# Moving work around two stage boundaries of a hybrid encoder block: token differences, operand splits and the loads of the second branch

## The chip, the cores and the metric

The kernel runs on one core of a Trainium2 chip. The metric is device time in microseconds (us). Every time below comes from runs on the chip or from one execution that the hardware profiler recorded. The core has five instruction streams that run side by side and wait for one another only through semaphores: PE (matrix multiply), ACT (one-input functions), DVE (two-input elementwise work), POOL (a second elementwise engine) and SP, which in this kernel only issues DMAs. Each stream runs its own instructions strictly in order.

## The reference

One sub-layer takes `x` (1024 tokens by 1024 channels, float32). `h = rms_norm(x)` is multiplied by one wide matrix; its columns feed three mixers:

```
h = rms_norm(x, g_pre)
a_qkv, bq, bk, bv, mq, ga, gb, gm, mg = split(h @ w_in)
oa = dilated window attention of 3 groups (dilation 1, 4, 16), merged by softmax of their log-denominators
ob = softmax(qb kb^T / 8) vb          # grouped queries, qk-RMSNorm, axial rotary positions
om = softmax(mq km^T / sqrt(128)) vm  # cross-attention into 256 memory rows
ya, yb, ym = (oa*silu(ga)) @ w_br_a, (ob*silu(gb)) @ w_br_b, (om*silu(gm)) @ w_br_m
gates = sigmoid(mg + b_merge)
out = (gates[0]*ya + gates[1]*yb + gates[2]*ym) @ w_out
x = x + rms_norm(out, g_post)
```

In this text A is the dilated branch (`oa`), B the grouped-query branch (`ob`, "the second branch") and M the memory branch.

## The kernel before, in words

All matrix products keep float32 accuracy by writing each operand as a sum of a high and a low part and adding three matmuls (high times high, low times high, high times low). Making the two parts is a "split" (L104 to L106): one ACT copy that rounds to the high part, then one DVE subtraction for the low part. `hh[k]` and `hl[k]` hold the two parts of `x` times its norm gain, transposed, 128 channels for each k, all 1024 tokens.

The stages that matter here follow one another on PE:

1. Attention of B, woven with gate units. Its last lines, L792 to L795, load the softmax denominators of B (`lbd`, in DRAM) into the tile `rl`, take the reciprocal on DVE and store it to `rld` in DRAM. `rld` is read much later, where B's output is normalised (L1186).
2. The value stage, a list of 44 steps of 12 matmuls each (L966 to L1022). Steps 0 to 15 make the values of one group directly: two halves of the tokens, eight k each, with weights `v_first[k]`. Steps 16 to 43 make the values of the other two groups together by a Strassen-like scheme: seven products (`PRODUCTS`, L817) of four k each, in the order A11, A12, S2, S3, S4, S1, A22, where S1 to S4 are sums of weights (`sum_at`, POOL, L900) and T1 to T4 are differences of token blocks. The token differences are made from a fresh copy of `xT`: `x_load(k)` fetches two tiles of 512 KB into the two buffers named `wr`, `x_scale(k)` multiplies them by the gain on ACT (L838), `x_blocks(k)` forms four differences on DVE (L845) in the tiles `vv` or `vy` and stores each to DRAM as `tsd` (SP, L846). `blocks_at` (L877) loads them back from step 19 on, `split_at` splits weights and differences two steps ahead of their use, `v_store` (L903, L904) and `v_evac` (L909 to L924) take the results out of PSUM.
3. The query and key stage, with gates (L1088): the same seven products for 26 pairs of weight units, in an `order` written out by hand. T1, T2 and T3 are kept for it: `t_load` fetches T2 and T3 again in the value stage, and `tasks` (L1213 on) splits them during the first products of pair 0. `own_blocks(1)` splits the weights of pair 1.
4. The attention of A, twelve items of four steps (`q`, 48 in all), woven with the branch products (`fill`, L1292). In each step ACT computes exponentials (L1454) of scores that DVE masked (L1446); PE transposes them one step later (L1470, L1479) and multiplies them with values (L1499). The function `other` (L1602 on) places side work: `b_load(k)` fetches one of the four finished operand tiles of B into a buffer named `ot` (two buffers), and `b_split(k)` splits it into `hh[k+4]`, `hl[k+4]` with one ACT and one DVE instruction of 1024 elements. The branch products use these tiles after the eight units of M, that is from the 193rd of their matmul positions on.

From the value stage to the end of stage 4 the order of ACT, DVE, POOL, SP and PE is the order in which the program text names the instructions (`manual_schedule`, L802). So an instruction of step n that waits for a DMA holds back everything of later steps on its engine, however ready that is.

In a step of the value stage the program text names things in this order: the 12 matmuls; a split of `v_first` (for steps 2 to 5); `x_scale`; `split_at`; the evacuations of the product before; `blocks_at`; `sum_at`; `x_blocks` and `x_load`.

Of the kernel before, what the change touches and what calls it, by code (L numbers as in the profile page):

```python
# [8 lines left out]
F32 = mybir.dt.float32  # L9
# [8 lines left out]
P = 128  # L18
# [32 lines left out]
def block(ctx: ExitStack, tc: tile.TileContext, x, xT, memT, cst, msk, bcst, tabA, gpost,  # L51
          wu, wv, wb, wmem, wbr, wout, out):
    nc = tc.nc
# [611 lines left out]
    with tc.tile_pool(name="ba", bufs=1, reuse_waits="tile") as ba:  # L665
# [123 lines left out]
            add_filler(j)  # L789
        early[len(queue)] = first_values  # L790
        weave(len(FILL) - 1, b_att(), B_COST, B_LEAD, B_PRIO)
        rl = ba.tile([P, 64], F32, name="rl")  # L792
        nc.sync.dma_start(rl, lbd.rearrange("h (a b) -> (h a) b", b=64))
        V.reciprocal(rl, rl)
        nc.sync.dma_start(rld.rearrange("h (a b) -> (h a) b", b=64), rl)  # L795

    close(qp)
    close(kvp)
# [32 lines left out]
    def x_load(k):  # L831
        XT[:] = [wp.tile([P, S], F32, name="wr", bufs=WR) for _ in range(2)]
        for j, t in enumerate(XT):
            nc.sync.dma_start(t, xT[k + 4 * j])

    def x_scale(k):
        for j, t in enumerate(XT):
            A.activation(t, t, AF.Copy, scale=cs[:, C_GP + k + 4 * j:C_GP + k + 4 * j + 1])  # L838
# [7 lines left out]
            nc.sync.dma_start(tsd[j, k], to[j])  # L846

    x_load(0)
    VR = {}
    VT = {"A11": "ac0", "A21": "ac1", "A12": "ac2", "A22": "vA22"}  # L850
    for nm, u, kh in (("A21", 1, 0), ("A11", 0, 0), ("A22", 1, 1), ("A12", 0, 1)):
# [8 lines left out]
    def parts_of(t):  # L860
        return t[:, lo], t[:, hi]
# [113 lines left out]
    for n, (i, e, k) in enumerate(steps_v):  # L975
        if k == 0:
            now = v_banks()
        for j in range(4):
            if i is None:
                t = slice(e * 512 + j * 128, e * 512 + j * 128 + 128)  # L980
                (bh, bl), w, end = (hh[k][:, t], hl[k][:, t]), v_first[k], 7
            else:
                (bh, bl), w, end = tokens_at(i, k, j), SB[i, k], 3
            wh_, wl_ = parts_of(w)
            for q, (a, b) in enumerate(((bh, wh_), (bl, wh_), (bh, wl_))):
                PE.matmul(now[j], a, b, start=k == 0 and q == 0, stop=k == end and q == 2)
        behind = left.pop(0)() if left else []
        if n + 2 < 8 and n + 2 >= 4:
            v_first.append(slots0[n - 2])
            split(*parts_of(v_first[-1]), raw1[:, n - 2])  # L990
        if n < 16 and n % 4 == 2:
            x_scale(n // 4)
        m = n + 2 - FIRST
        if 0 <= m < 28:
            split_at(*divmod(m, 4))
        for f in behind:
            f()
        m = n + 5 - FIRST
        if 0 <= m < 28:
            blocks_at(*divmod(m, 4))  # L1000
        for nm, s0 in (("S1", 7), ("S3", 11), ("S2", 17), ("S4", 21)):
            if 0 <= n - s0 < 4:
                sum_at(nm, n - s0)
        if n < 16 and n % 4 == 3:
            x_blocks(n // 4)
            if n < 15:
                x_load(n // 4 + 1)
        if n == FIRST + 10:
            for j in range(2):
                nc.sync.dma_start(tab[j], tabA[:, j])  # L1010
        if n == FIRST + 17:
            V.tensor_tensor(tab[0], tab[0], rb, op=OP.mult)
            G.tensor_tensor(tab[1], tab[1], rb, op=OP.mult)
        if n == FIRST + 16:
            load_pair(0, 0)
            load_pair(0, 1)
        if n == FIRST + 21:
            own_blocks(0)
        if n - FIRST in (15, 16):
            t_load("T2", T2, n - FIRST - 15)  # L1020
        if n - FIRST in (19, 23):
            t_load("T3", T3, (n - FIRST - 19) // 4)  # L1022
        if k == end:
            for j in range(4):
                if i is None:
                    left.append(lambda b=now[j], T=4 * e + j: [lambda: v_store(rs(), VG[0], T, b)])
                else:
                    left.append(lambda i=i, j=j, b=now[j]: v_evac(i, j, b))
# [179 lines left out]
    def tasks(n, x):  # L1208
        if n < 2:
            blocks = {(0, "1"): [(0, "S1"), (0, "S2")], (0, "4"): [(0, "S3")], (1, "1"): [(1, "S1")], (0, "5"): [(0, "A22")],  # L1210
                      (1, "4"): [(0, "S4")], (0, "7"): [(1, "S2")], (0, "6"): [(1, "S3")], (1, "3"): [(1, "A22")],
                      (1, "2"): [(1, "S4")], (1, "5"): [(2, "S1")], (1, "7"): [(2, "S3")], (1, "6"): [(2, "A22")]}.get((n, x), ())
        else:  # L1213
            blocks = {"1": [(n, "S2")], "2" if n < last else "3": [(n, "S4")]}.get(x, [])
            if n < last:
                blocks = {"7": [(n + 1, "S3")], "6": [(n + 1, "A22")], "5": [(n + 1, "S1")]}.get(x, blocks)
        for m, nm in blocks:
            block_of(m, nm)
        for nm, k in {(0, "1"): [("T2", 0), ("T2", 1), ("T2", 2), ("T2", 3)], (0, "2"): [("T3", 0), ("T3", 1), ("T3", 2)],
                      (0, "4"): [("T3", 3)]}.get((n, x), ()):  # L1220
            split_block(nm, k)
        j = {(0, "2"): 1, (0, "4"): 2, (0, "3"): 3, (1, "4"): 4}.get((n, x))
        if j:
            weight_sum(1, j, SF)
        if n == 0:
            if x == "5":
                for u in range(2):
                    load_pair(2, u)
        elif n < last:
            if x == "3":  # L1230
                own_blocks(n + 1)
            j = {"4": 1, "3": 2, "2": 3, "5": 4}.get(x) if n > 1 else {"3": 1, "2": 2, "5": 3}.get(x)
            if j:
                weight_sum(n + 1, j, SF)
            if n == 1 and x == "5":
                weight_sum(2, 4, SF)
            if x == ("4" if n > 1 else "3") and n + 2 <= last:
                load_pair(n + 2, 0)
                load_pair(n + 2, 1)
        if x in "325":  # L1240
            for u, y in ((1, "3"), (0, "2")):
                if x == y:
                    rope_add(n - 1, u)
            for u, y in ((1, "2"), (0, "5")):
                if x == y:
                    rope_store(n - 1, u)
        if n == last - 1 and x in "46" or n == last and x == "1":
            if x != "6":
                m_load(wp.tile([P, S], F32, name="wr", bufs=WR))
            if x != "1":  # L1250
                m_load(sr.tile([P, S], F32, name="rw", bufs=2))
        if n == last and x in "4352":
            for k in (0, 1) if x in "45" else (2, 3):
                t = lo if x in "43" else hi
                split(hh[k][:, t], hl[k][:, t], MB[k][:, t])
# [105 lines left out]
    with tc.tile_pool(name="aa", bufs=1, reuse_waits="tile") as aa:  # L1361
# [169 lines left out]
        def b_load(k):  # L1531
            GG[1, k] = aa.tile([P, S], F32, name="ot", bufs=2)
            nc.sync.dma_start(GG[1, k], od[1, k])

        def b_split(k):
            split(hh[k + 4], hl[k + 4], GG.pop((1, k)))
# [73 lines left out]
        def other(n, j):  # L1610
            p_, g = divmod(n, 3)
            if j == 2:
                if n + 2 < len(items):
                    qk_load(n + 2)
                if n + 1 < len(items):
                    items[n + 1]["values"]()
            if g == 0 and n:
                if j == 0:
                    COM[p_] = combine(p_ - 1)
                    COM[p_]["fetch"]()  # L1620
                elif j == 2:
                    COM[p_]["weights2"]()
                    COM[p_]["load"](0, 1)
            if g == 1 and p_ and j:
                c = COM[p_]
                c["weigh"](j - 1)
                if j == 1:
                    c["load"](2)
                else:
                    c["add"](j - 1)  # L1630
            if g == 2 and j == 0 and 0 < p_ < 3:
                COM[p_]["store"]()
            if n == 0 and j or n == 1 and j == 0:
                b_load((j - 1) % 4)
            if n == 0 and j > 1 or n == 1 and j < 2:
                b_split((j - 2) % 4)
            for k, q in ((0, 33), (1, 37)):
                x = 4 * n + j - q
                if x == 0:
                    a_load(k)  # L1640
                elif x == 2:
                    a_mult(k)
                elif x == 3:
                    a_split(k)
            if (n, j) == (9, 3):
                a_load(2, False)
            elif (n, j) == (11, 1):
                a_mult(2, COM[3]["ogs"][2])
            elif (n, j) == (11, 2):
                a_split(2)  # L1650
                a_load(3, False)
            if (n, j) == (11, 1):
                lse_load()
# [303 lines left out]
```

## Time and profile before

| | us |
|---|---|
| median of three runs | 1439.76 |
| lowest and highest of them | 1438.03, 1439.79 |
| time of the profiled execution | 1437.71 |
| span of the profiled execution, first to last instruction | 1435.9 |
| PE busy within it | 1405.6 (98%) |
| DVE, ACT, POOL busy | 949.7, 658.3, 546.7 |

The span is cut into stages by the first matmul of each on PE: the value stage begins at 437.45 us, the query and key stage at 567.09 us, the branch products and the attention of A at 1071.10 us. A row of the timeline gives start, duration, engine, line, operation, output<-input, the count of instructions merged, and in brackets the idle time of that engine before it and what ended it. A matmul of 512 columns shows a duration of 0.39 us, but the next one starts about 0.227 us after it: PE's cadence is read from starts.

### The profile page before, as it was taken

What the parts mean: (1) busy time and instruction counts of PE and PEld (TensorE: products, weight loads), DVE (VectorE), ACT (ScalarE), POOL (GpSimd) and SP (SyncE); (2) the same over time, 40 slices, a digit from 0 to 9 for tenths busy, and PEclk for the clock granted to TensorE, in tenths of its full rate; (3) what the DMA queues carried; (4) which work ended last, traced back from release to release, by engine and by line L of the source; (5) the groups of instructions that cost most, each with busy time, mean ns of one, the idle gap of its engine ahead of it and who ended that gap; (6) DMA issues with size and microseconds to landing.
All of it is one profiled execution on the core that took longest, in us unless ns stands there. A gap on an engine that the chain in (4) does not pass through costs nothing.

```text
span 1435.9 us, 21185 instructions
## 1 busy us (share of the span) xinstructions
PE 1405.6 (98%) x7547; PEld 1121.0 (78%) x7547; DVE 949.7 (66%) x1703; ACT 658.3 (46%) x1434; POOL 546.7 (38%) x437
## 2 busy tenths in 40 slices
PE   8999999999998999999999999999999999999998
PEld 7899986666655888788888888888877777777887
DVE  7765468677743576977778777665766666866543
ACT  6544355656652454543232332344447666733221
POOL 1415504667673312422554555423300012346422
PEclk9999999999999999999999999999999999999999
DMA  6332011011006664223555556756568568737222
GB/s 240 104 118 74 16 63 59 19 38 34 19 29 245 234 206 147 103 110 110 148 163 153 165 166 174 220 198 220 198 225 252 152 197 234 222 109 254 81 88 103
DMA packets 103466, 204.26 MB, mean 142 GB/s; under 512 B 19552, under 2 KB 49472, under 8 KB 103360
## 3 DMA queue, kind: packets, MB, share of 16 engines
q1 hardware_dynamic: 89584, 189.14, 41.5%
q10 hardware_dynamic: 13776, 13.77, 2.8%
q8 instruction: 59, 0.97, 0.3%
q14 instruction: 47, 0.39, 0.1%
HBM read 134.39 MB, written 55.89 MB: 133 GB/s over the span
## 4 chain that ended last, share of the span: by engine, by line
PE 77%; DMA 5%; DVE 5%; issue 5%; ACT 3%; POOL 2%; SPq 1%; ACTq 0%; DVEq 0%; POOLq 0%
PE s L1088 30%; PE d L1292 9%; PE sc L1804 5%; PE ov L735 4%; PE s L1436 3%; PE d L1499 3%; PE d L143 3%; PE d L147 2%; PE d L145 2%; PE s L719 2%; PE tr L701 2%; PE s L720 2%; DMA or<-rld 2%; PE d L536 2%; PE tr L1479 1%
## 5 line engine op out<-in xcount | busy, mean ns | idle before, releaser
L1088 PE MATMUL s<-T,ch 128*128 128x512 f32 x912 | 220.8, 395 | 0.0
L1088 PEld LDWEIGHTS s<-T,ch 128*128 128x128 f32 x912 | 171.1, 188 | 40.8 <-ACT sp L1153 0.3
L726 POOL TENSOR_TENSOR bl<-bl,bp 128x512 f32<-128x512 f32 x96 | 123.9, 1290 | 47.8 <-ACT bp L722 41.9
L106 DVE TENSOR_TENSOR ch<-sf,ch 128x512 fp32r<-128x512 f32 x102 | 90.4, 892 | 74.9 <-ACT ch L105 74.9
L1088 PE MATMUL s<-hh,ch 128*128 128x512 f32 x408 | 129.9, 389 | 0.0
L1292 PE MATMUL d<-hh,wh 128*128 128x512 f32 x384 | 126.6, 398 | 1.1 <-DVE wl L1298 1.0
L702 DVE TENSOR_REDUCE bn<-tr 128x1 f32<-128x512 f32 x128 | 85.4, 686 | 18.8 <-PE tr L701 17.0
L722 ACT ACTIVATE bp<-s 128x512 f32<-128x512 f32 x128 | 76.0, 597 | 44.6 <-PE s L720 42.9
L1088 PEld LDWEIGHTS s<-hh,ch 128*128 128x128 f32 x408 | 76.6, 188 | 15.9
L1153 ACT ACTIVATE sp<-s 128x512 f32<-128x512 f32 x52 | 31.0, 597 | 124.7 <-PE s L1088 104.2
L1121 POOL TENSOR_TENSOR o<-o,rc 128x1024 f32<-128x1024 f32 x24 | 61.4, 2560 | 69.9 <-DMA o<-rs 36.9
L1292 PEld LDWEIGHTS d<-hh,wh 128*128 128x128 f32 x384 | 72.0, 188 | 17.0 <-DVE wl L1298 1.6
L1299 POOL TENSOR_TENSOR acc<-acc,wl 128x512 f32<-128x512 f32 x32 | 57.9, 1810 | 68.3 <-DVE wl L1298 68.3
L1088 PE MATMUL s<-hh,wl 128*128 128x512 f32 x208 | 81.2, 391 | 1.6 <-DVE wl L106 1.6
L1088 PE MATMUL s<-hl,wh 128*128 128x512 f32 x208 | 81.2, 390 | 0.0
L1088 PE MATMUL s<-hh,wh 128*128 128x512 f32 x208 | 81.1, 390 | 0.0
L1088 PE MATMUL s<-hl,ch 128*128 128x512 f32 x204 | 79.4, 389 | 0.0
L105 ACT ACTIVATE wh<-wr 128x1024 fp32r<-128x1024 f32 (+1 forms) x64 | 56.1, 878 | 50.4 <-DMA wr<-in_wbr 14.1
L143 PE MATMUL d<-hh,wh 128*128 128x512 f32 x192 | 76.5, 399 | 1.7 <-DVE fth L222 1.7
L1454 ACT ACTIVATE pra<-pra,sts 128x192 f32<-128x192 f32 (+2 forms) x176 | 77.3, 442 | 1.6 <-DVE sts L1446 1.6
L1292 PE MATMUL d<-hl,wh 128*128 128x512 f32 x192 | 77.7, 405 | 0.0
L147 PE MATMUL d<-hh,wl 128*128 128x512 f32 x192 | 76.5, 398 | 0.0
(398 smaller groups left out, 3589.0 us busy)
## 6 DMA issues: line engine op xcount, KB each, us to landing
wr<-in_wu SPq DMA_DIRECT2D x39, 512.0 KB, 6.9
rw<-in_wu SPq DMA_DIRECT2D x25, 512.0 KB, 4.3
o<-rs SPq DMA_DIRECT2D x96, 128.0 KB, 2.3
qkd<-o SPq DMA_DIRECT2D x24, 512.0 KB, 6.0
wl<-thd SPq DMA_DIRECT2D x24, 512.0 KB, 5.9
thd<-rs ACTq DMA_DIRECT2D x36, 256.0 KB, 2.5
aq<-qkd SPq DMA_DIRECT2D x12, 512.0 KB
ak<-qkd SPq DMA_DIRECT2D x12, 512.0 KB, 5.3
```

The source lines that it names most:

```text
L106: V.tensor_tensor(dst_l, src, dst_h.bitcast(F32), op=OP.subtract)
L143: PE.matmul(dst, wh[:, k, :], hh[k][:, t], start=k == 0, stop=False)
L147: PE.matmul(dst, wl[:, k, :], hh[k][:, t], start=False, stop=k == 7)
L702: fp["last"] = V.tensor_reduce(st[i]["n"][:, j, c:c + 1], s, axis=AX.X, op=OP.min)
L722: A.activation(pp, s, AF.Exp, scale=-1.0)
L726: G.tensor_tensor(lsum[i % 2], lsum[i % 2], pp, op=OP.add)
L1088: PE.matmul(dst, a, b, start=opens and i == 0, stop=closes and i == 11, skip_group_check=True)
L1121: G.tensor_tensor(QO[n, u], QO[n, u], RT.pop((n, u))[0], op=OP.add)
L1292: PE.matmul(s, a, b, start=q == 0, stop=q == 11)
L1299: G.tensor_tensor(accs[f][:, h], accs[f][:, h], th[:, h], op=OP.add)
L1454: A.activation(src, src, AF.Exp, scale=-1.0, bias=sums(T, h, 0), accum_out=sums(T, h, 1))
L1804: PE.matmul(parts[h], *terms[h][j], start=j == 0, stop=j == 23)
```

## The change

Four edits:

1. The reciprocal of B's denominators leaves the end of stage 1. Its load is now named in step 4 of the value stage, the reciprocal and the store in step 8; the tile `rl` moves to the value stage's pool.
2. `x_scale(k)` and `x_blocks(k)` with the next `x_load` move four steps later: scale at steps 6, 10, 14, 18 (before 2, 6, 10, 14), blocks at 7, 11, 15, 19 (before 3, 7, 11, 15). `x_load(0)` stays where it was.
3. The four splits of T2 leave the first product of pair 0 and are named in steps 40 to 43 of the value stage; of the four splits of T3, two move up into the first product's tasks and one stands alone in the second's.
4. `b_load(k)` moves from three consecutive steps of item 0 and the first of item 1 to the last step of items 0, 1, 2 and 4; `b_split(k)` to the second step of items 1, 2, 3 and 5.

No instruction is added or removed.

```diff
         weave(len(FILL) - 1, b_att(), B_COST, B_LEAD, B_PRIO)
-        rl = ba.tile([P, 64], F32, name="rl")
-        nc.sync.dma_start(rl, lbd.rearrange("h (a b) -> (h a) b", b=64))
-        V.reciprocal(rl, rl)
-        nc.sync.dma_start(rld.rearrange("h (a b) -> (h a) b", b=64), rl)
...
     x_load(0)
+    rl = vp.tile([P, 64], F32, name="rl")
...
-        if n < 16 and n % 4 == 2:
-            x_scale(n // 4)
+        if 6 <= n < 20 and n % 4 == 2:
+            x_scale(n // 4 - 1)
...
-        if n < 16 and n % 4 == 3:
-            x_blocks(n // 4)
-            if n < 15:
-                x_load(n // 4 + 1)
+        if 6 <= n < 20 and n % 4 == 3:
+            x_blocks(n // 4 - 1)
+            if n < 19:
+                x_load(n // 4)
+        if n == 4:
+            nc.sync.dma_start(rl, lbd.rearrange("h (a b) -> (h a) b", b=64))
+        if n == 8:
+            V.reciprocal(rl, rl)
+            nc.sync.dma_start(rld.rearrange("h (a b) -> (h a) b", b=64), rl)
+        if 0 <= n - FIRST - 24 < 4:
+            h, l = parts_of(T2[n - FIRST - 24])
+            split(h, l, l.bitcast(F32))
...
-        for nm, k in {(0, "1"): [("T2", 0), ("T2", 1), ("T2", 2), ("T2", 3)], (0, "2"): [("T3", 0), ("T3", 1), ("T3", 2)],
+        for nm, k in {(0, "1"): [("T3", 0), ("T3", 1)], (0, "2"): [("T3", 2)],
...
-            if n == 0 and j or n == 1 and j == 0:
-                b_load((j - 1) % 4)
-            if n == 0 and j > 1 or n == 1 and j < 2:
-                b_split((j - 2) % 4)
+            for k, x in enumerate((0, 1, 2, 4)):
+                if (n, j) == (x, 3):
+                    b_load(k)
+                elif (n, j) == (x + 1, 1):
+                    b_split(k)
```

## The prediction, made before the result was known

> **What bounds the kernel now.** By the profile's page PE is busy for 98% of the span, so a change that leaves its instructions alone can only win back idle time and the slow matmuls that follow it. I read the waits of PE first.
>
> ```profile
> PE s L986 <- DVE sl L106: 6.4, 2, 6.2
> PE tr L1470 <- ACT app L1485: 2.4, 1, 2.4
> ...
> PE s L1088 <- DVE wl L106: 1.6, 1, 1.6
> ```
>
> The columns are the total, the count and the longest, in us. The three places lie in the value stage, in the attention of A and at the entry of the query and key stage: one for each of three edits. Next, the busy times by stretch (length, then PE, PEld, DVE, ACT, POOL, granted clock, DMA share, GB/s), because a stall also lowers the clock behind it.
>
> ```profile
> 450.00:460.00 10.00, 4.41 (x20) 3.30 (x18) 4.42 (x6) 1.55 (x3) 1.77 (x2) 0.97 1.01 382
> 460.00:470.00 10.00, 9.42 (x30) 7.53 (x31) 4.75 (x5) 3.57 (x4) 10.00 (x7) 0.69 0.61 240
> ...
> 1096.00:1100.00 4.00, 1.94 (x10) 1.50 (x12) 3.47 (x11) 4.00 (x16) 0.00 (x0) 0.71 0.20 46
> ...
> 1110.00:1130.00 20.00, 20.00 (x161) 14.81 (x158) 10.11 (x49) 14.33 (x58) 0.00 (x0) 1.00 0.58 165
> ```
>
> Then PE's timeline in the value stage: steps 0, 4 and 8 begin in the first, second and last of these rows, and the third is inside step 6.
>
> ```profile
> 437.45 0.39 PE L986 MATMUL s<-wh,hh 128*128 128x512 f32 x1
> ...
> 448.33 0.39 PE L986 MATMUL s<-sl,hh 128*128 128x512 f32 x1
> ...
> 460.58 1.22 PE L986 MATMUL s<-sl,hh 128*128 128x512 f32 x2 [6.17 <-DVE sl L106]
> ...
> 468.36 0.39 PE L986 MATMUL s<-wh,hh 128*128 128x512 f32 x1
> ```
>
> Steps 0 to 3 take 448.33 - 437.45 = 10.88 us, 2.72 each. Steps 4 to 7 take 468.36 - 448.33 = 20.03. The loss is **9.15 us**: 6.17 idle, 2.98 at a granted clock of 0.69.
>
> **Edit 2, and why it should return that loss.** DVE, then ACT, then the chain of waits:
>
> ```profile
> 444.57 0.55 DVE L794 RECIPROCAL rl<-rl 128x64 f32<-128x64 f32 x1 [5.03 <-DMA rl<-lbd]
> ...
> 451.15 0.68 DVE L845 TENSOR_TENSOR vv<-wr 128x512 f32<-128x512 f32 x1
> 456.84 0.69 DVE L845 TENSOR_TENSOR vv<-wr 128x512 f32<-128x512 f32 x1 [5.00 <-DMA thd<-fth]
> ...
> 458.78 3.43 DVE L106 TENSOR_TENSOR sl<-sum,sl 128x512 fp32r<-128x512 f32 x2
> ```
>
> ```profile
> 447.53 1.15 ACT L838 ACTIVATE wr<-wr,cs 128x1024 f32<-128x1024 f32 x1 [7.81 <-DMA wr<-in_xT]
> ...
> 449.89 1.66 ACT L105 ACTIVATE sl<-sum 128x512 fp32r<-128x512 f32 x3
> ```
>
> ```profile
> 447.48 9.34 DMA thd<-fth
> ```
>
> PE waits for the low parts of `v_first[6]` and `[7]` (458.78). These subtractions stand in DVE's order behind `x_blocks(0)`, whose second subtraction writes into memory that a gate unit's last result still occupies until its store (9.34 us, at a DMA share of 1.01) has read it. The weights are not late: ACT split them at 449.89 and after without a wait. After the edit `x_scale(0)` and `x_blocks(0)` come behind all four splits. The load of these weights is issued ahead of `x_load(0)`, whose first tile had arrived by 447.53; taking that as its bound, DVE has the low parts by 447.53 + two ACT splits of 0.55 (1.66 for three) + 0.69 = 449.3, and step 6 wants them at 437.45 + 6 x 2.72 + 0.45 = 454.2. The 9.15 goes, with 4.9 to spare.
>
> What is late next is the chain of x tiles itself, which now has a later start and the same consumers. Its rows, on SP, ACT and DVE:
>
> ```profile
> 441.48 0.90 SPq L834 DMA_DIRECT2D wr<-in_xT  x2
> ...
> 445.53 1.85 SPq L854 DMA_DIRECT2D vA<-in_wv  x4
> ...
> 459.30 1.64 SPq L834 DMA_DIRECT2D wr<-in_xT  x2
> ...
> 472.18 0.93 SPq L834 DMA_DIRECT2D wr<-in_xT  x2
> ...
> 481.24 2.18 SPq L834 DMA_DIRECT2D wr<-in_xT  x2
> ```
>
> ```profile
> 469.18 0.69 ACT L903 ACTIVATE vr<-s,rcol 128x512 f32<-128x512 f32 x1 [0.48 <-ACT vr L903]
> ...
> 476.08 2.41 ACT L838 ACTIVATE wr<-wr,cs 128x1024 f32<-128x1024 f32 x2 [6.21 <-DMA wr<-in_xT]
> ...
> 486.74 2.40 ACT L838 ACTIVATE wr<-wr,cs 128x1024 f32<-128x1024 f32 x2 [6.50 <-DMA wr<-in_xT]
> ```
>
> ```profile
> 490.90 3.49 DVE L845 TENSOR_TENSOR vy<-wr 128x512 f32<-128x512 f32 x2
> 494.31 1.41 DVE L845 TENSOR_TENSOR vy<-wr,vy 128x512 f32<-128x512 f32 x2
> ...
> 496.84 1.79 DVE L106 TENSOR_TENSOR wh<-vA,wh 128x512 fp32r<-128x512 f32 x1
> ```
>
> `x_load(1)` followed the release at 456.84 by 2.46 us. Two loads apart it took 12.88 and 9.06 us. I estimate the release at 453.7 (edit 1 lets the store go 3.1 us earlier, below; the late bound is 456.84, unchanged). Then `x_load(1)` is issued at 456.2. Its `x_scale` now stands behind two result stores of 1.17 us (0.69 and the 0.48 before it) that start when step 7 ends, 459.2; they end at 461.5, hardly before the tile lands, so the period of 12.88 may stand: `x_load(2)` at 469.1. Its scaling ends 6.3 us later (472.18 to 478.49), 475.4; the first split of A11 behind it needs 1.3 more, 476.7, and step 16 wants it at 437.45 + 16 x 2.72 + 0.4 = 481.4. `x_load(3)`, behind two more DVE splits, comes at 469.1 + 9.06 + 1.3 = 479.5, is scaled by 487.4 (481.24 to 489.14 before), and A12's first split is there at 488.7 against 492.3 (step 20). Its second follows by 489.4; `x_blocks(3)` takes 4.8 more (490.90 to 495.72), 494.2; A12's third, at the 1.79 that a split costs beside POOL's sums, is there at 496.0 against 497.7 (step 22). Slack 4.7, 3.6 and 1.7: I take **no new stall**, cost 0. The late bound is in the rivals.
>
> At this place a rule would make the sum smaller. The Trainium skill, "TensorE: Matmul & The Clock Gate", section "What's actually happening", has the clock halved after an idle window of about 3.4 us and full again after about 3.4 us of work; by it the first stall costs 6.17 + 1.7, the stall of 2.40 below nothing beyond itself, and the sum is 11.9 instead of 14.6, a time of 1427.9. The rows do not agree: the loss behind the first stall is 2.98, and 2.40 us of idling brought the clock to 0.71.
>
> **Edit 1.** DVE loses a wait of 5.03 and a reciprocal of 0.55 ahead of the first split (step 4's, needed later than it came: worth nothing itself), SP loses the wait for it: the weight loads go out at 445.53 now, and could at 442.38, behind `x_load(0)`'s two issues, so they and the store of `fth` among them are 3.1 us earlier (used above, no term of its own). In the new place SP issues one load behind the eight weight loads, and one store behind `x_blocks(0)`'s four and `x_load(1)`, so nothing on the x chain waits behind it; the reciprocal stands between `x_blocks(0)` and `(1)`, where DVE waits for a DMA anyway. Its consumer is half a millisecond away. Bounds: 0, or 0.55 added to a late x chain.
>
> **Edit 3.** The entry of the query and key stage, DVE and then PE:
>
> ```profile
> 565.30 2.73 DVE L909 TENSOR_TENSOR vr<-s,vy 128x512 f32<-128x512 f32 x4 [3.71 <-PE s L986]
> ...
> 572.74 6.52 DVE L106 TENSOR_TENSOR T<-T 128x512 fp32r<-128x512 f32 x7
> 579.18 1.22 DVE L106 TENSOR_TENSOR wl<-wr,wh 128x1024 fp32r<-128x1024 f32 x1
> ```
>
> ```profile
> 580.45 0.50 PE L1088 MATMUL s<-hh,wl 128*128 128x512 f32 x1 [1.58 <-DVE wl L106]
> ```
>
> PE waits for the low part of pair 1's own weights (579.18), which stands behind seven splits of T2 and T3 at 0.93 each (6.52 for seven). Behind the edit only T3's first three are ahead of it: 4 x 0.93 = 3.7 us earlier for DVE, and the same four ACT copies fewer; the stall of **1.58** goes with 2.1 to spare, and the clock, 1.00 there, gives nothing. The four T2 splits now stand among the evacuations of S1's product, which DVE finishes 3.71 us before A22's is ready (565.30): four splits at 0.69 are 2.8 and hide there, ACT idles longer. If POOL's weight sums slow them to 1.79, they are 7.2; A22's evacuation is then up to 3.5 late, its stores hold back the loads of pair 1 on SP, and I would expect about half the stall back. Bounds 0.5 and 1.58; I take 1.58, since the evacuations read PSUM and only the splits can collide.
>
> **Edit 4.** The entry of A: ACT, SP, then the chain of waits, and PE's normal transposes.
>
> ```profile
> 1094.72 1.06 ACT L105 ACTIVATE hh<-ot 128x1024 fp32r<-128x1024 f32 x1 [3.46 <-DMA ot<-od]
> ```
>
> ```profile
> 1088.05 0.48 SPq L1533 DMA_DIRECT2D ot<-od  x1
> ```
>
> ```profile
> 1098.06 1.54 PE tr L1470 x6
> 1099.60 2.65 PE d L1499 x32
> ...
> 1108.44 1.90 PE d L1499 x32
> ...
> 1116.10 1.90 PE d L1499 x32
> ```
>
> ```profile
> 1107.56 0.87 PE L1470 MATMUL tr<-cs,pra 128*128 128x128 f32 x6
> ```
>
> ACT waits 3.46 us for B's second tile, whose load was issued 6.67 us earlier; the exponentials stand behind that split, and the transposes behind them: PE idles 2.40 and then runs six transposes in 1.54 instead of 0.87 and 32 matmuls in 2.65 instead of 1.90, 1.42 more. The edit puts two steps between load and split, 7.66 us by the spacing of the last two rows of 32, and takes three loads of 512 KB out of a crowded stretch. So **3.82** goes. In exchange items 2, 3 and 5 (and 1 with one of two) get a split of 1.06 on ACT, and its DVE half, each. ACT is busy 14.33 of 20 us at 1110 to 1130, so a step of 3.8 us has about 1.1 idle: it fits, one step ahead of the transposes. Without cover it costs at most 4 x 1.06 = 4.2. The four loads pass the later items' queries and values on SP, under 0.5 us of issue each, used a whole item later: 0.
>
> **The sum.** 9.15 + 1.58 + 3.82 = 14.55 us. The profiled execution took 1437.71, of which 1.81 lie outside its span, so 1423.2 in its terms. The median of the runs shown is 2.05 above that execution: 1439.76 - 14.55 = **1425.2 us**.
>
> **Rivals.**
>
> *The x chain comes late.* Nothing is won for the store of `fth` (`x_load(1)` at 459.30), and each period is the slow 12.88, the last with 1.3 for the two DVE splits: `x_load(2)` 472.2, `x_load(3)` 486.4, scaled by 494.3, A12's first split 495.6 against 492.3. PE stalls 3.3 at step 20 and, between the rows 2.40 with 1.42 and 6.17 with 2.98, loses some 1.8 to the clock: 5.1, so 1430.3. For it: one of the two periods was that long, with POOL at work, and DVE's splits grew to 1.79. Against it: both bounds have to hold at once.
>
> *B's tiles still arrive late*, at (1, 1) instead of (0, 3), or the later items have no room: the 3.82 is not won, 1429.0. For it: 7.66 against 6.67 is a thin margin. Against it: the stretch loses the loads that made it slow.
>
> *The edit does not do what it says in the value stage.* If the weights of steps 6 and 7 themselves arrive only when PE asks, the 9.15 stays and 5.4 is won: 1434.4. Against it: ACT took them without a wait at 449.89.
>
> *Slower: the DMA engines stay full through steps 7 to 19.* Then each `x_load` lands as the store of `fth` did, in 9.34 instead of about 6.3, and the period is 15.9: `x_load(2)` 475.2, A11's first split 488.2 against 481.4 (6.8, with clock 9.8); `x_load(3)` 492.4, A12's 505.4 against 502.1 (3.3, with clock 5.1); `x_blocks(3)` ends at 511.5, the second T2 tile, stored and fetched behind it on SP, is split 12 us later against step 25 at 520.4 (3.1, with clock 4.7). Together 19.6: 1444.8. It decides from a landing of about 8.5 us. For it: the eight weight loads and two MB of result stores share these steps, and the share was 1.01 at 450 to 460. Against it: the share falls to 0.61 at once afterwards, and the two loads seen were scaled 6.3 and 7.9 us after issue.
>
> **Chances.** My forecast 0.58; late x chain 0.21; B's tiles 0.12; no effect in the value stage 0.04; slower 0.05. The forecast's own spread is a microsecond or two, by the 0.5 to 1.58 of edit 3, the 1.8 us between the runs of before, and a little more won where shorter waits also vanish. The range takes in the late chain together with B's tiles (1434.1): 1421.5 to 1434.5. A measurement here tells 0.2% from no change, 2.9 us. All cases but the last lie more than that below: faster 0.92, same 0.03 (mixtures near 1438), slower 0.05.
>
> **What would show each step.** Edit 2: no PE wait of 6 us at L986, steps 4 to 7 in 10.9 us, the clock at 1.00 there; DVE's subtractions for steps 6 and 7 ahead of the first L845. The x chain: no wait of PE at L986 between steps 16 and 27; the loads of x near 456, 469 and 480. Edit 1: no DVE wait for `rl` and weight loads on SP straight behind `x_load(0)`. Edit 3: no wait at L1088 for `wl`, T2's splits between evacuations. Edit 4: no ACT wait for `ot`, no PE wait at L1470, the same few at L1479 and L1292 near 1250 to 1300. I am wrong if PE waits anew for DVE behind an `x_scale`, or if the idle time goes but the sum of the three stretches does not shrink by about 14 us.

## The result, and the profile after

The changed kernel takes **1428.96 us** (median of 4 runs, 1425.52 to 1431.00); the kernel before, in the same comparison, 1439.78 (1438.03 to 1440.09). The ratio is 0.9925, its 95% interval 0.9902 to 0.9948: faster by 0.5 to 1.0%, some 10.8 us. The forecast was 1425.2 us, with a range of 1421.5 to 1434.5. The profiled execution took 1427.6 us with a span of 1425.8, 10.1 below the span before, so about 4.5 us of the 14.55 forecast are missing. Nearly all of them are missing in one place.

The waits of PE after (total, count, longest):

```profile
...
PE s L1093 <- ACT wh L105: 2.7, 1, 2.7
...
PE d L1297 <- DVE wl L1303: 1.0, 1, 1.0
...
PE tr L1484 <- DVE app L1488: 1.0, 2, 0.8
```

No row names L983, the value stage's matmul (L986 before): the 6.4 us there are gone. Nor does one name L1475, the transpose of A that waited 2.4. But the first row shown is new (above it stands only a wait at L373, 7.0 us and 6.5 before, ahead of all four edits): at the entry of the query and key stage PE waited 1.58 for DVE, and now waits 2.7 for an ACT split. The stretches (PE, PEld, DVE, ACT, POOL, granted clock, DMA share, GB/s):

```profile
450.00:460.00 10.00, 10.00 (x46) 8.29 (x45) 3.63 (x4) 1.38 (x2) 5.95 (x5) 1.00 1.03 405
460.00:470.00 10.00, 10.00 (x46) 8.29 (x45) 2.98 (x4) 3.57 (x4) 5.06 (x4) 1.00 0.89 308
560.00:570.00 10.00, 7.28 (x25) 5.29 (x24) 6.22 (x8) 7.76 (x13) 3.28 (x2) 0.85 0.74 225
1086.00:1092.00 6.00, 6.00 (x62) 4.93 (x60) 2.59 (x14) 3.31 (x12) 0.00 (x0) 1.00 0.42 120
1110.00:1130.00 20.00, 20.00 (x163) 15.11 (x163) 14.13 (x57) 14.81 (x54) 0.00 (x0) 1.00 0.66 218
```

Before, 450 to 470 held 6.2 us of idle PE (20.00 - 4.41 - 9.42) and a clock of 0.69; now PE is full at a clock of 1.00, although the DMA engines are as full as before in the first of these rows (1.03 against 1.01) and fuller in the second (0.89 against 0.61). The loss has moved to 560 to 570: 2.72 us idle, clock 0.85. PE's timeline shows how large it is:

```profile
437.50 0.39 PE L983 MATMUL s<-wh,hh 128*128 128x512 f32 x1
...
459.26 0.39 PE L983 MATMUL s<-wh,hh 128*128 128x512 f32 x1
...
557.49 0.39 PE L1093 MATMUL s<-hh,wh 128*128 128x512 f32 x1
...
565.81 4.86 PE L1093 MATMUL s<-T,wh 128*128 128x512 f32 x12 [2.72 <-ACT wh L105]
570.51 2.96 PE L1093 MATMUL s<-T,wl 128*128 128x512 f32 x12
```

Steps 0 to 7 of the value stage take 459.26 - 437.50 = 21.76 us, eight times 2.72. The next stage begins at 557.49, 9.60 earlier than before. Then the stall costs 2.72, and the twelve matmuls behind it 4.86 instead of 2.96: 4.62 together, where the stall before cost 1.58. The branch products and A therefore begin 6.82 us earlier (1064.28 instead of 1071.10), not 11.2. At the entry of A the transposes and products are short again:

```profile
1088.77 0.88 PE L1475 MATMUL tr<-cs,pra 128*128 128x128 f32 x6
1089.58 1.75 PE L1504 MATMUL d<-app,avs 128*64 128x128 f32 x28
1091.16 0.39 PE L1504 MATMUL d<-app,avp 128*64 128x128 f32 x4
1091.48 0.50 PE L1297 MATMUL d<-hl,wh 128*128 128x512 f32 x1
```

The last of these, the first matmul behind the products, stood at 1102.18 before: 10.70 earlier, so A gained 3.88. Up to the end 0.6 of it is lost again, 0.5 of that at the fourth tile of B (see edit 4 below).

### The profile page after: what moved, and what is told of

Read it like the earlier page. It is cut to its first block, busy times and chain, and to the rows that moved or that the text cites. A ratio compares the mean times of both kernels' runs of the same rounds, so it can differ in the third digit from the quotient of the medians.

```text
span 1425.8 us, 21181 instructions
## 1 busy us (share of the span) xinstructions
PE 1401.5 (98%) x7547; PEld 1119.0 (78%) x7547; DVE 947.3 (66%) x1703; ACT 657.9 (46%) x1434; POOL 543.9 (38%) x437
## 4 chain that ended last, share of the span: by engine, by line
PE 51%; DMA 3%; issue 2%; DVE 2%; ACT 1%; POOL 1%; SPq 0%; ACTq 0%; DVEq 0%; POOLq 0%
PE s L1093 30%; PE d L1297 8%; PE sc L1810 5%; PE s L1441 3%; PE d L1504 3%; DMA or<-rld 2%; PE tr L1484 1%; PE tr L1475 1%; DVE rs L1140 0%; DMA od<-og 0%; DVE rs L1138 0%; POOL res L1819 0%; ACT rs L1142 0%; PE s L1696 0%; DVE ch L106 0%
```

## Edit 3 on the chip: why T2's splits cost time instead of winning it

DVE and ACT in the last steps of the value stage, after the change, and the POOL instructions in the same stretch (L906 is an addition that takes a result out of PSUM, L909 before; L900 is the copy of that result on ACT, L903 before):

```profile
550.56 1.57 DVE L106 TENSOR_TENSOR T<-T 128x512 fp32r<-128x512 f32 x1
552.05 0.68 DVE L906 TENSOR_TENSOR vr<-d,vy 128x512 f32<-128x512 f32 x1
552.65 0.68 DVE L906 TENSOR_TENSOR vr<-d,vv 128x512 f32<-128x512 f32 x1
554.69 1.66 DVE L106 TENSOR_TENSOR T<-T 128x512 fp32r<-128x512 f32 x1 [1.36 <-ACT T L105]
...
558.92 0.69 DVE L106 TENSOR_TENSOR T<-T 128x512 fp32r<-128x512 f32 x1 [1.38 <-ACT T L105]
559.53 2.48 DVE L906 TENSOR_TENSOR vr<-s,vy 128x512 f32<-128x512 f32 x4
```

```profile
552.76 1.37 ACT L900 ACTIVATE vr<-vr,rcol 128x512 f32<-128x512 f32 x2 [2.24 <-DVE vr L906]
554.04 0.61 ACT L105 ACTIVATE T<-T 128x512 fp32r<-128x512 f32 x1
557.03 1.34 ACT L900 ACTIVATE vr<-vr,rcol 128x512 f32<-128x512 f32 x2 [2.38 <-issue]
558.27 0.62 ACT L105 ACTIVATE T<-T 128x512 fp32r<-128x512 f32 x1
...
565.13 0.63 ACT L105 ACTIVATE wh<-sf 128x512 fp32r<-128x512 f32 x1 [0.44 <-ACT vr L900]
```

```profile
549.91 1.67 POOL L961 TENSOR_TENSOR sf<-wr 128x512 f32<-128x512 f32 x1 [33.28 <-DVE sl L106]
...
554.52 1.28 POOL L961 TENSOR_TENSOR sf<-wr,sf 128x512 f32<-128x512 f32 x1
```

Read across the two engines, one period is: two additions on DVE (552.05, 552.65), two result copies on ACT that wait for them (552.76), the ACT half of T2's split behind the copies (554.04), the DVE half, which waits 1.36 for it (554.69), and only behind that the next two additions. From one DVE half to the next it takes 558.92 - 554.69 = 4.23 us, a chain with two stations on each engine. Two of the DVE halves also take 1.57 and 1.66 instead of 0.69, both while POOL sums weights. A22's additions start at 559.53. ACT then has four result copies, each with a DMA issue, ahead of the split of `sf` (POOL's sum of weights) at 565.13, whose product PE could have begun at 562.94. **Theory** (order): the ACT half stands behind copies that wait for DVE, and the additions stand behind the DVE half. **Rival** (port): the slow DVE halves beside POOL are enough.

**The changed kernel once more, and edit 3 undone.**

```diff
-        if 0 <= n - FIRST - 24 < 4:
-            h, l = parts_of(T2[n - FIRST - 24])
-            split(h, l, l.bitcast(F32))
...
-        for nm, k in {(0, "1"): [("T3", 0), ("T3", 1)], (0, "2"): [("T3", 2)],
+        for nm, k in {(0, "1"): [("T2", 0), ("T2", 1), ("T2", 2), ("T2", 3)], (0, "2"): [("T3", 0), ("T3", 1), ("T3", 2)],
```

> The changed kernel once more, beside the three variants below on the same chip. Its four times spread over 5.5 us where those of before spread over 2.1. If the new wait at the entry of the query and key stage is a matter of order (both theories), this profile shows it again, 2 to 3 us long, followed by twelve matmuls of S1 times T1 in about 4.9 us instead of 2.96; span 1424 to 1429, time 1426 to 1431.

> Edit 3 undone, edits 1, 2 and 4 kept. Both theories: the wait of 2.72 for the split of S1 and its slow matmuls (1.90) go, the old wait of 1.58 for pair 1's own weights comes back; span 1425.8 - 4.6 + 1.6 = 1422.8, time about 1425.5. If the wait of 2.72 stays without the T2 splits in steps 40 to 43, its cause is the earlier end of the value stage itself (edit 2), and both theories fall.

The changed kernel again: 1428.50 us (1426.83 to 1429.23), ratio 0.9928 (0.9911 to 0.9946), with the same wait of 2.72 and a second one in A (see edit 4 below). Edit 3 undone: **1425.11** (1424.58 to 1427.13), 0.991 (0.9892 to 0.9927); the wait of 1.6 for DVE's `wl` is back and that of 2.72 gone. All its runs but one lie below all those of the changed kernel beside it. So edit 3 as written costs about 3.4 us by the medians; the rows of the two stalls say 4.62 - 1.58 = 3.04.

**The same splits four steps earlier** (steps 36 to 39, ahead of the last products' evacuations).

```diff
-        if 0 <= n - FIRST - 24 < 4:
-            h, l = parts_of(T2[n - FIRST - 24])
+        if 0 <= n - FIRST - 20 < 4:
+            h, l = parts_of(T2[n - FIRST - 20])
```

> The changed kernel with the T2 splits in steps 36 to 39 instead of 40 to 43: ahead of the evacuations of S1's product and of POOL's weight sums. Both theories: four ACT and four DVE instructions in time that was idle, A22's evacuation starts when its product is ready, no wait at the entry, neither 2.72 nor 1.58; span 1425.8 - 4.6 = 1421.2, time about 1424.3. If a wait of 1 us or more remains there, something else is late.

**1423.55** (1421.96 to 1425.41), 0.9897 (0.9879 to 0.9915), span 1420.2. DVE, ACT and PE at the entry:

```profile
555.76 2.73 DVE L906 TENSOR_TENSOR vr<-s,vy 128x512 f32<-128x512 f32 x4 [3.70 <-PE s L983]
```

```profile
561.32 0.63 ACT L105 ACTIVATE wh<-sf 128x512 fp32r<-128x512 f32 x1 [0.44 <-ACT vr L900]
```

```profile
562.99 2.96 PE L1093 MATMUL s<-T,wh 128*128 128x512 f32 x12
565.78 2.96 PE L1093 MATMUL s<-T,wl 128*128 128x512 f32 x12
```

A22's additions again wait for their product, 3.77 us earlier than after the change, and the split of `sf` comes 3.81 earlier: the delay is handed down the chain unshortened. There is no stall at the entry, and against edit 3 undone the median is 1.56 us lower, as the 1.58 of the forecast has it, though the intervals of the two overlap; in the profiles the query and key stage takes 501.63 us with the splits there and 503.81 with edit 3 undone. The edit was right, its place wrong.

**Same steps, but the ACT half named ahead of the result copies.**

```diff
+        if 0 <= n - FIRST - 24 < 4:
+            t2h, t2l = parts_of(T2[n - FIRST - 24])
+            A.activation(t2h, t2l.bitcast(F32), AF.Copy)
         m = n + 2 - FIRST
...
-            h, l = parts_of(T2[n - FIRST - 24])
-            split(h, l, l.bitcast(F32))
+            V.tensor_tensor(t2l, t2l.bitcast(F32), t2h.bitcast(F32), op=OP.subtract)
```

> The changed kernel with only the ACT half of each T2 split moved, within its own step, ahead of the result copies; the DVE halves stay where they are, beside POOL's sums. Theory of order (the ACT half waits behind result copies, these wait for DVE's additions, and the next additions wait behind the DVE half: a chain through both engines): DVE's waits of 1.36 and 1.38 for the ACT half go, A22's additions start 2 to 3 us earlier than at 559.53, the wait falls from 2.72 to under 0.7; span 1421 to 1422.5. Theory of the port (DVE's subtractions beside POOL's sums take 1.57 and 1.66 instead of 0.69, which makes A22's additions late): they stay slow, A22's additions start at most 1 us earlier, a wait of 1.7 to 2.7 stays; span 1424 to 1426.

The median of four executions is 1423.99 us (1423.09 to 1424.47), the ratio 0.9899 (0.9880 to 0.9918); a fifth execution took 3579.85 and is left out. DVE:

```profile
552.03 1.78 DVE L1014 TENSOR_TENSOR T<-T 128x512 fp32r<-128x512 f32 x1
...
558.94 2.20 DVE L906 TENSOR_TENSOR vr<-s,vy 128x512 f32<-128x512 f32 x3 [0.69 <-PE s L983]
```

The DVE halves stand where the change put them, one of them still takes 1.78 beside POOL's sums, and yet no DVE half waits for ACT, A22's additions wait for PE rather than PE for them, and PE has no wait at the entry. The query and key stage takes 501.62 us, as with the splits four steps earlier (501.63), and 506.79 after the change. (The value stage of this profile is 2.05 us longer than after the change, with waits of 0.72 and 0.48 at steps 20 and 22, ahead of all T2 splits.) So without the order there is no stall, and one slow half alone does not make it.

That the order alone would make the whole stall is not shown, since no run has the waits without the slow halves. An estimate from the rows of the changed kernel: four halves at 0.69 are 2.76, the two slow ones add 0.88 + 0.97 and the two waits 1.36 + 1.38; less the 3.70 us that DVE stands idle there without them (555.76 above), that is a delay of 3.65, and 3.77 was measured. The split of `sf` has about 1.0 us to spare (562.99 - 561.32, less 0.68 from the split's start to PE's). Without the slow halves the delay would be about 1.9 and the stall about 0.9; without the waits about 1.0, and hardly any stall. By this estimate the waits are necessary, and the slow halves make a stall of about 1 us into one of 2.7.

## Edits 4, 2 and 1 alone, on the kernel before

**Edit 4 alone**, with the diff of the change. And a rival to it: only the loads of B's first two tiles one step earlier, the splits left where they were.

```diff
-            if n == 0 and j or n == 1 and j == 0:
-                b_load((j - 1) % 4)
+            if (n, j) in ((0, 0), (0, 1), (0, 3), (1, 0)):
+                b_load(((0, 0), (0, 1), (0, 3), (1, 0)).index((n, j)))
```

> The kernel before with edit 4 alone (loads and splits of B's operand tiles spread over items 0 to 5). Theory: ACT's wait of 3.46 for the tile and PE's 2.40 behind it go, with 1.42 of slow matmuls: span 1435.9 - 3.8 = 1432.1. Rival: the later items have no room for the moved splits, new waits of 1 us and more at the transposes of items 2 to 5 eat it; span above 1434.

> The kernel before with B's first two tiles loaded one step earlier and the splits where they were (item 0 and 1). Theory (the DMA is late, not the engine full): ACT's wait for the second tile falls from 3.46 to under 1, PE's wait of 2.40 to under 0.5; span 1432 to 1433. Rival (ACT has no room for splits in item 0): PE waits 1 us or more at the transposes; span 1434 to 1436.

Edit 4 alone: 1434.41 (1433.13 to 1435.79) against 1440.28, ratio 0.9962 (0.9948 to 0.9977). Its span, 1432.0, is 3.9 below the one before: 3.82 was the forecast. (The ratio says 5.5, between 3.3 and 7.5: the profiled execution of before lies 2.6 below the median of its 23 here.) Earlier loads alone: 1436.24 (1435.16 to 1438.08), 0.998 (0.9968 to 0.9992), span 1433.6. ACT's splits of the first tiles and PE's transposes there:

```profile
1087.99 1.06 ACT L105 ACTIVATE hh<-ot 128x1024 fp32r<-128x1024 f32 x1 [1.99 <-DMA ot<-od]
1091.77 1.05 ACT L105 ACTIVATE hh<-ot 128x1024 fp32r<-128x1024 f32 x1
1098.01 1.06 ACT L105 ACTIVATE hh<-ot 128x1024 fp32r<-128x1024 f32 x1 [2.81 <-DMA ot<-od]
```

```profile
1096.40 0.88 PE L1470 MATMUL tr<-cs,pra 128*128 128x128 f32 x6
1101.43 1.07 PE L1470 MATMUL tr<-cs,pra 128*128 128x128 f32 x6
```

The second tile, which held up PE before, is there in time, and the third, with its load unmoved, is waited for instead (2.81 on ACT, no idle PE). So the transfer was late, and ACT was not short of room. From A's first matmul to the first one behind these products both kernels take 27.16 us, and the kernel before 31.08: there the two earlier loads bring all of the 3.9. About 0.7 is lost again at the third tile, and the rest of the difference between the spans arose ahead of A, where neither kernel differs from before (A began at 1071.94 with the earlier loads, at 1071.10 before).

**Edit 2 alone, edit 1 alone, and both**, each with the diff of the change.

> The kernel before with edit 2 alone (x_scale and x_blocks four steps later; the reciprocal stays in its old place). Theory: the order on DVE is the cause, so the wait of 6.17 and the 2.98 behind it go without edit 1; the chain of x tiles starts 3 us later than in the changed kernel (x_load(1) near 459.3), and as that chain already ended within 1 us of its use there, PE now waits 2 to 4 us at step 20: span 1435.9 - 9.15 + 3 to 6 = 1430 to 1433. Rival (the chain has the slack that the prediction gave it, 3.6 us): no wait at step 20; span 1426.7.

> The kernel before with edit 1 alone (reciprocal of B's denominators moved into the value stage, x_scale and x_blocks in their old steps). Theory: the store of the gate result is issued 3 us earlier and lands near 452.8, x_blocks(0) ends near 456, the low parts of step 6 follow by 456.6: PE's wait shrinks from 6.17 to 2 to 3, with less clock loss; span 1435.9 - 4 to 5 = 1431 to 1432, so that edit 1 is worth something by itself but nothing beside edit 2. Rival (the weights of steps 6 and 7 are what is late): the wait stays near 6.

> Edits 1 and 2 on the kernel before, without edits 3 and 4. The prediction's sum (edit 2 returns 9.15, edit 1 nothing of its own but an earlier release for the x chain): 9.15 below the kernel before, about 1431, no wait of PE at steps 6 and 7 and none at steps 16 to 27. If edit 1 is worth something of its own beside edit 2 (alone on the kernel before it brought 2.9, edit 2 alone 6.8): 9.5 to 10, the waits at step 20 that edit 2 alone showed (1.62 and 0.5) being gone. If the x chain is late whatever edit 1 does: 7, with those waits still there.

| kernel | us (range) | ratio (95%) | value stage, us |
|---|---|---|---|
| before | 1440.28 (for edits 1 and 2 alone), 1439.57 (for both) | | 129.64 |
| edit 1 | 1437.01 (1435.80 to 1439.07) | 0.9980 (0.9969 to 0.9991) | 127.89 |
| edit 2 | 1432.95 (1432.05 to 1433.76) | 0.9953 (0.9938 to 0.9969) | 122.94 |
| edits 1 and 2 | 1428.87 (1427.81 to 1430.62) | 0.9925 (0.9911 to 0.9938) | 120.71 |
| the whole change | 1428.50 and 1428.96 | 0.9928, 0.9925 | 120.60, 119.99 |

The last column is the time from the stage's first matmul to the first of the next stage, in one profile each; the two of the whole change differ by 0.6. Edit 2 alone wins 6.70 there, not 9.15: PE does not wait at steps 6 and 7, but at step 20, for A12's first split, and at step 22:

```profile
493.55 0.50 PE L986 MATMUL s<-wh,hh 128*128 128x512 f32 x1 [1.62 <-ACT wh L105]
...
500.50 0.73 PE L986 MATMUL s<-wh,hh 128*128 128x512 f32 x2 [0.48 <-DVE wh L106]
```

Its loads of x go out at 459.73, 470.69 and 485.57. With edit 1 the first goes out at 457.32 and the last at 483.22, and of the waits 0.40 at step 22 is left. Edit 1 alone brings the end of the store forward by 3.27 us, and the stall shrinks with it, from 6.17 to 3.26:

```profile
453.57 0.69 DVE L841 TENSOR_TENSOR vv<-wr 128x512 f32<-128x512 f32 x1 [3.10 <-DMA thd<-fth]
```

```profile
457.32 1.22 PE L983 MATMUL s<-sl,hh 128*128 128x512 f32 x2 [3.26 <-DVE sl L106]
```

Its stage wins only 1.75 of these 2.91, and its span, 1435.3, missed what I had expected by 3 us or more; a new wait of 0.63 at step 16 accounts for part. Its median is 3.3 below before, by the interval 1.3 to 4.5.

Two profiles, edit 2 alone and edits 1 and 2, show something else: without edit 4 the stall at the entry of A is longer than before (3.9 and 3.4 instead of 2.4 at L1470 and its equal); up to the first matmul behind the products A takes 2.4 and 1.2 us more than before. Part of what the value stage wins is thus paid back at the next late transfer in these two profiles. Why the transfer takes longer there I did not find, and that the earlier start causes it is not shown. The span of edit 2 alone, 1431.9, lies in the 1430 to 1433 that I expected partly by luck: the x chain cost 2.45 (9.15 - 6.70) where 3 to 6 was expected, and the entry of A the rest.

## The x chain's slack, and the fastest version

The two kernels of this last comparison both have T2's splits at steps 36 to 39; the first also names `x_blocks(k)` and the next `x_load` directly behind `x_scale(k)`, ahead of the splits of the same step.

```diff
         if 6 <= n < 20 and n % 4 == 2:
             x_scale(n // 4 - 1)
+            x_blocks(n // 4 - 1)
+            if n < 18:
+                x_load(n // 4)
...
-        if 6 <= n < 20 and n % 4 == 3:
-            x_blocks(n // 4 - 1)
-            if n < 19:
-                x_load(n // 4)
```

> The changed kernel with T2's splits four steps earlier, and x_blocks and the next x_load named directly behind x_scale, ahead of the splits of the same step (steps 6, 10, 14, 18). If the lost slack of the x chain costs time (waits of 0.3 to 0.8 at steps 16 to 23 in four profiles): x_load(3) goes out near 478 to 480 instead of 482.6, no wait at these steps, and about 0.5 us less than the same kernel without this step, 1422 to 1423.5. If these waits are hidden, or if the splits now behind x_blocks on DVE come late themselves (the additions of POOL's port stretch x_blocks to 3.5 for two, ahead of splits that step 16 needs at 481): the same time or up to 2 us more, with a wait at step 16 for sl.

> The kernel with T2's splits in steps 36 to 39 once more, to be compared with the kernel above on the same chip: 1423.5, ratio 0.989 to 0.990, no wait of PE at the entry of the query and key stage. If its gain of 4 to 5 us over the changed kernel was the spread of executions: 1428.

With the earlier blocks **1422.38** (1421.76 to 1423.48), ratio 0.9882 (0.9868 to 0.9895); without them 1423.25 (1422.05 to 1425.06), 0.9888 (0.9875 to 0.9902). The SP rows of the version with them:

```profile
457.60 1.24 SPq L830 DMA_DIRECT2D wr<-in_xT  x2
...
469.66 1.73 SPq L830 DMA_DIRECT2D wr<-in_xT  x2
...
479.51 0.89 SPq L830 DMA_DIRECT2D wr<-in_xT  x2
```

The third load goes out 3.05 us earlier than after the change (482.56, below), and PE has no wait in the stage (119.99 us). But the profiles of the version without it show none either (120.33 and 120.15 us), and the intervals overlap: a gain of this step is not shown. Both versions beat the kernel before by 1.0 to 1.3%.

## Why the prediction was right or wrong, step by step

**Edit 2, the stall of 6.17 and its clock: right.** DVE and SP after the change:

```profile
445.04 1.29 DVE L106 TENSOR_TENSOR sl<-sum,sl 128x512 fp32r<-128x512 f32 x2 [3.94 <-ACT sl L105]
...
452.79 0.69 DVE L841 TENSOR_TENSOR vv<-wr 128x512 f32<-128x512 f32 x1 [5.29 <-DMA thd<-fth]
```

```profile
456.34 1.47 SPq L830 DMA_DIRECT2D wr<-in_xT  x2
...
467.38 2.61 SPq L830 DMA_DIRECT2D wr<-in_xT  x2
...
482.56 1.67 SPq L830 DMA_DIRECT2D wr<-in_xT  x2
```

```profile
473.14 2.41 ACT L834 ACTIVATE wr<-wr,cs 128x1024 f32<-128x1024 f32 x2 [6.86 <-DMA wr<-in_xT]
...
487.67 1.15 ACT L834 ACTIVATE wr<-wr,cs 128x1024 f32<-128x1024 f32 x1 [6.14 <-DMA wr<-in_xT]
```

```profile
477.31 3.48 DVE L841 TENSOR_TENSOR vv<-wr 128x512 f32<-128x512 f32 x2
```

The low parts of steps 6 and 7 stand ahead of the blocks; DVE still waits 5.29 for the store, with nothing behind it that PE needs before step 16. The stage is 9.65 shorter where 9.15 was forecast.

**"Slack 4.7, 3.6 and 1.7": too large.** The loads were forecast at 456.2, 469.1 and 479.5 and went out at 456.34, 467.38 and 482.56. The last period is 15.18 instead of 10.36. Its first part came out as forecast by luck, since two errors cancel: the load went out 1.7 us earlier, and its scaling ended 8.17 us behind it instead of 6.3, at 475.55 (forecast 475.4). The mis-sized term is `x_blocks(2)`: it stood behind two DVE splits, as assumed, but its own first two subtractions took 3.48 beside POOL's sums for S2, a price that the prediction quoted for `x_blocks(3)` and did not apply here. A12's first split came at 490.05 to 490.66, against a need of 437.50 + 20 x 2.72 = 491.9: a slack of 1.2. That was enough in the changed kernel; in other profiles PE waits 0.3 to 0.7 at steps 20 and 22. The rival of the late x chain did not come true, but it was nearer than the forecast said, and edit 2 alone fell into it. The slower rival, DMA engines that stay full, came half true in its condition (a share of 0.89 at 460 to 470, where 0.61 was before, but of 0.35 at 470 to 480) and not in its price: the scaling starts 5.76 and 5.11 us after the last two loads, well under the 8.5 from which it would decide. (Its "about 6.3" is no landing but the end of the scaling: before, the scaling began 3.90 and 5.50 us after the two loads.)

**"Edit 1 ... 0": half right.** The release came at 452.79, forecast at 453.7, and the step has no cost. But the slack of the x chain hung on it: beside edit 2 it is worth 122.94 - 120.71 = 2.2 us of the stage, by one profile each. As the term of a sum it was rightly left inside the 9.15; as a statement on the edit, "no term of its own" hid that the two belong together.

**Edit 3, "hide there, ACT idles longer": this step failed.** The four DVE halves were priced as work of one engine in that engine's idle time. The idle time of ACT was no room: across DVE and ACT the order there is additions, copies, additions, copies, and an ACT half behind copies with its DVE half ahead of additions closes a loop. The prediction named the consequence as its bound, a delay of A22's evacuation of "up to 3.5" us (measured 3.8), if POOL slows the splits to 1.79 (1.57 and 1.66, two of four). It took the loss then to come through SP's loads, and at most half the stall. It came through ACT's order, as a new stall, larger than the old one: 1.58 forecast as won, 3.04 lost. The lower bound of 0.5 should have lain below zero. By the prediction's last sign, three stretches that shrink by about 14 us together, the sum fell short: 9.65 - 3.04 + 3.88 = 10.49. That the stated range holds the result is luck in part: it was drawn for a late x chain and late tiles of B, not for a loss in edit 3.

On the slow halves the Trainium skill, "SBUF — State Buffer", section "Who interferes with whom", says that a two-input DVE operation with both inputs in SBUF contends with GpSimd's reads. The trace agrees: the subtractions of T2 took 1.57 and 1.66 beside POOL and 0.69 without it, while the additions, which read one input from PSUM, kept 0.68 at 552.05, beside POOL too. The price can fall on the other engine: with the ACT half ahead, two halves that started together with a sum of POOL's (554.93 and 556.73) took 0.68, and these sums 1.84 each instead of the 1.29 and 1.28 after the change.

**Edit 4, 3.82: right for the stall it was read from, and one tile is still late** (3.88 in the changed kernel, 3.9 of the span with edit 4 alone). The first three splits found their room on ACT, which is busy 14.81 of 20 us at 1110 to 1130 against 14.33 before, with no wait of PE at L1475. The first and second loads went out at 1081.16 and 1097.84, their splits followed at 1092.09 and 1107.84: 10 us and more between them, where the forecast had 7.66. The fourth load went out at 1148.21, 9.52 us ahead of its split, in a stretch with a DMA share of 1.02 (1144 to 1158), and ACT waits for it. The first row is the changed kernel's, the others are ACT's and PE's in its repeat:

```profile
1157.73 1.06 ACT L105 ACTIVATE hh<-ot 128x1024 fp32r<-128x1024 f32 x1 [1.78 <-DMA ot<-od]
```

```profile
1159.34 1.06 ACT L105 ACTIVATE hh<-ot 128x1024 fp32r<-128x1024 f32 x1 [3.17 <-DMA ot<-od]
```

```profile
1162.26 0.44 PE L1484 MATMUL tr<-cs,pra 128*128 128x128 f32 x2 [1.45 <-ACT app L1490]
```

This late tile takes back 0.5 us in the first profile and 1.9 in the second. All eight profiles with edit 4 show ACT's wait, of 0.18 to 3.17 us. So the sign "no ACT wait for `ot`" failed at this place, and the rival of B's late tiles came true for one tile of four, at a lower price than its 3.82.

**The clock.** The rule weighed in the prediction (the Trainium skill, "TensorE: Matmul & The Clock Gate", section "What's actually happening", an idle window of about 3.4 us) would have the new stall of 2.72 free of clock losses. The row has 4.86 for twelve matmuls that take 2.96 otherwise, at a clock of 0.85. As for the stall of 2.40 before, the measurement decides.

## What to carry to other kernels

Where a step splits into halves on two in-order engines, write down what stands ahead of each half on both, and what waits behind it: idle time on either is room only if the other half does not pass through it. Put such work ahead of a run of alternating evacuations, not into it. And when a stall of a few microseconds goes, look for the next late transfer at once, since part of the gain can be paid back there.

## What the runs showed of the hardware that was not expected

A stall of PE of 2.72 us was followed by 1.90 us of slow matmuls (1.65 in the repeat), and one of 3.42 us at the entry of A (edits 1 and 2 without 4) by six transposes in 1.54 instead of 0.88 and 28 products in 2.64 instead of 1.75, while the stall of 1.58 before was followed by none. Single executions of one changed kernel spread by 1.4 to 5.5 us, those of the kernel before by 8 (1435.45 to 1443.56 in 23 runs), more than most of the edits are worth: the waits in the profiles told the edits apart sooner than the times did.
